# A dense half-group between the two directions' scores of an RWKV-7 scan, and four shared PSUM banks for its small products

## The chip, the cores and the metric

The kernel runs on one core of a Trainium2 chip. Its time is the device time of one execution in microseconds (us), and it was run three times. TensorE is called PE below, VectorE DVE, ScalarE ACT, GpSimd POOL, and SP is the engine that issues most DMAs.

## The reference

One layer of a bidirectional hybrid encoder, 1024 tokens of 1024 channels, float32: half a SwiGLU feed-forward, a mixer, half a second SwiGLU, and a last norm. The mixer projects its input once and feeds two branches, a gated long convolution (Hyena) and an RWKV-7 scan in two directions. Cut to the part that matters here:

```
h = _rmsnorm(x, mix_norm)
u_hy, u_rw, g_hy, g_rw = jnp.split(h @ w_in, split_at, axis=-1)
y_hy = _hyena_branch(u_hy, ...)          # ends in z @ hy_out
y_rw = _rwkv7_branch(u_rw, ...)          # ends in y @ rw_out
merged = jax.nn.sigmoid(g_hy) * y_hy + jax.nn.sigmoid(g_rw) * y_rw
x = x + merged @ w_out

def _rwkv7_step(S, inp):                 # 8 heads of 64, two directions, 1024 steps
    r, w, k, v, kk, a = inp
    sa = jnp.einsum('dbhij,dbhj->dbhi', S, -kk)
    S = S * w[..., None, :] + sa[..., None] * (kk * a)[..., None, :] + v[..., None] * k[..., None, :]
    y = jnp.einsum('dbhij,dbhj->dbhi', S, r)
```

After the scan, the two directions' outputs are added, normed for each head, given a bonus term and multiplied by a gate g.

## The kernel before, in words

The scan is computed in 8 blocks of 128 tokens (`NB`), each two chunks of 64, both directions `d` at once, as products of small matrices. `Rwkv.run` (line 1103) is a Python generator: each `yield` is a place where the caller may put other work of PE. For one block its stretches are, in this order:

- `transposes` of `BT` and the products `pv` for both directions (lines 1141 to 1145), then `ws` with the loads of the next block's `prep`, then `us`, `r` and `ms`;
- `scores` of the next block (line 923): for each direction two pairs of banks, each filled by products of `BK` and `T3` and read by DVE, which multiplies them by a mask into `rw_SC` (line 939); then `eliminate`, some forty short instructions of DVE that invert the triangular parts and end in the transposes of lines 980 and 982, the last writing `rw_xt`;
- `scan`, two chunks with the running state `rw_s`;
- `invert`, in four stretches: three products of `merge` need what ACT or DVE made of the product before (`rw_xt`, `rw_z`, `rw_lt`), and beside them stand the transposes to `rw_AV` and, in the third and fourth, the products of `rates` (tiles `rw_sg` and `rw_tha`) for the block after the next.

All these small products write one-bank tiles of one PSUM pool, `psA` (line 827), taken in turn from 3 buffers: a product that comes to a buffer waits until ACT or DVE has read the tile that was there. PSUM has 8 banks of 2 KB for each partition; the scan's pools hold 5 of them.

PE's other work is long dense matmuls, 128x512. Matmuls of the scan, the gates and Hyena's projection are kept in program order (`InOrder`, line 48), so where the generators yield sets PE's order; the other engines' order is made by a scheduler. Two callers fill the yields:

- `mixer_gates` (line 1362): 32 groups of 24 matmuls into `pw` (pool `mhp`, 3 banks), which yields in the middle and at the end of each, so 64 half-groups of 12; line 1644 takes one step of the scan after each. They last through the scan's preparation, blocks 0 to 4, and the first block's wait for `eliminate`.
- then, for blocks 5, 6 and 7, the loop at line 1655, which after each step of the scan may take a step of `RwkvPost.unit` (norm, bonus and gate of what the scan has finished; four steps a unit; its PSUM tiles come from 2 banks of a pool of their own, `rpp`) and a group of 12 matmuls of `hyena_out` into `pz` (1 bank). The residues of `i` modulo 10 say at which of a block's ten steps each of them stands.

The weights of the dense groups come by DMA into `w_st`, are rounded by ACT into `w_hi` (line 33), and DVE makes the rest, `w_lo` (line 37). ACT reads a finished gate group with a tanh into `mh_o`.

Of the kernel before, what the change touches and what calls it, by code (L numbers as in the profile page):

```python
# [17 lines left out]
PSUM = bass.MemoryType.PSUM  # L18
# [791 lines left out]
class Rwkv:  # L810
# [6 lines left out]
    def __init__(self, tc, ctx, I, dr, ident):  # L817
        self.tc, self.nc, self.I, self.dr, self.ident = tc, tc.nc, I, dr, ident
        self.te = InOrder(tc)
        nc = self.nc  # L820
        pool = lambda name, bufs, **k: ctx.enter_context(tc.tile_pool(name=name, bufs=bufs, **k))
        one = self.one = pool("rw1", 1)
        self.ld = pool("rwl", 2)
        self.el = pool("rwe", 2)
        self.mid = pool("rwm", 2)
        self.tp = pool("rwt", 1)
        self.psa = pool("rwpa", 3, space=PSUM)
        self.pss = pool("rwps", 1, space=PSUM)
        self.psy = pool("rwpy", 1, space=PSUM)

        def const(name, src, *shape):
            t = one.tile([P, *shape], F32, name=name)
            nc.sync.dma_start(t, src)
            return t

        self.w2 = const("rw_w2", I["rw_w2"].rearrange("d r c -> (d r) c"), 512)
        self.a2 = const("rw_a2", I["rw_a2"].rearrange("d r c -> (d r) c"), 512)
        self.start = const("rw_start", I["c_start"], 512)
        self.mask = const("rw_mask", I["c_mask"], 2 * CH)
        self.half = const("rw_half", I["c_half"], 2)  # L840
        self.eye = const("rw_eye", I["c_eye"], 16, 16)
        v = self.vec = one.tile([P, 4, 6], F32, name="rw_vec")
        for j, ap in enumerate((I["rw_w0"][0], I["rw_w0"][1], I["rw_a0"][0], I["rw_a0"][1], I["rw_k_a"])):
            nc.sync.dma_start(v[:, :, j], ap.rearrange("(t p) -> p t", p=P))
        nc.vector.tensor_scalar(v[:, :, 0:5], v[:, :, 0:5], 0.5, None, ALU.mult)
        nc.vector.tensor_scalar(v[:, :, 5], v[:, :, 4], -1.0, 1.0, ALU.mult, ALU.add)
        self.id2 = one.tile([P, CH], F32, name="rw_id2")
        for e in range(2):
            nc.vector.tensor_copy(self.id2[64 * e : 64 * e + 64], ident[64 * e : 64 * e + 64, 64 * e : 64 * e + 64])
        self.PP = [one.tile([P, 8, CH + 1], F32, name=f"rw_pp{d}") for d in range(2)]  # L850
        for t in self.PP:
            nc.vector.memset(t[:, :, 0:1], 1.0)
        self.TT = one.tile([P, 16, CH], F32, name="rw_tt")
        nc.gpsimd.memset(self.TT, 0.0)
        self.Z1 = one.tile([P, 16, 32], F32, name="rw_z1")
        nc.vector.memset(self.Z1, 0.0)
        self.quads = [(e, hb, 64 * e + 32 * hb) for e in range(2) for hb in range(2)]
        self.S = self.mid.tile([P, 8, 64], F32, name="rw_s")
        nc.vector.memset(self.S, 0.0)
# [63 lines left out]
    def scores(self, b):  # L923

        nc = self.nc
        fe = [slice(0, 64), slice(64, 128)]
        m = self.mask.unsqueeze(1).to_broadcast([P, 4, 2 * CH])
        for d in range(2):
# [3 lines left out]
            for h in range(2):  # L932
# [4 lines left out]
                                       T3[fe[e], 4 * h + i, e :: 2 - e], start=True, stop=True)  # L937
                for e in range(2):
                    nc.vector.tensor_tensor(SC[e][:, ts(h, 4)], ps[e], m, ALU.mult)

    def transposes(self, b, d, n):

# [160 lines left out]
    def run(self):  # L1103
# [23 lines left out]
        c = new(0)  # L1127
# [3 lines left out]
            self.prep(c, d)  # L1131
        for _ in range(5):
            yield
        self.scores(c)
        self.eliminate(c)
        for _ in range(5):
            yield
        x = yield from invert(c, 1)
        for s in range(NB):
# [15 lines left out]
            ms()  # L1155
            yield
            if x is not None:
                self.scores(x)
                self.eliminate(x)
                yield  # L1160
            yield from self.scan(c)
            if x is not None:
                c, x = x, (yield from invert(x, s + 2))
# [198 lines left out]
def mixer_gates(tc, I, wp, hA, hctx, hB, dr):  # L1362


    nc, te = tc.nc, InOrder(tc)
    with ExitStack() as ctx:
        pool = lambda name, bufs, **k: ctx.enter_context(tc.tile_pool(name=name, bufs=bufs, side="right", **k))
        ev = pool("mhe", 2)
        pw = ctx.enter_context(tc.tile_pool(name="mhp", bufs=3, space=PSUM))
        for t in range(2):  # L1370
            if t:
                for k in range(KD):
# [207 lines left out]
def hybrid_layer_kernel(ctx: ExitStack, tc: tile.TileContext, I: dict, out: bass.AP):  # L1580
# [58 lines left out]
    early = ExitStack()  # L1639
    right = lambda name, bufs: early.enter_context(tc.tile_pool(name=name, bufs=bufs, side="right"))  # L1640
    with ExitStack() as c2:
        rw = Rwkv(tc, c2, I, dr, ident).run()
        for _ in mixer_gates(tc, I, wp, h0, hctx, hB, dr):
            next(rw)
        with ExitStack() as c3:
            zp, z2, one, work = [right(n, b) for n, b in (("zz1", 1), ("zz2", 1), ("rp1", 1), ("rp2", 1))]
            pz, pq = [c3.enter_context(tc.tile_pool(name=n, bufs=b, space=PSUM)) for n, b in (("zzp", 1), ("rpp", 2))]
            hy = hyena_out(tc, I, wp, zp, z2, pz, dr)
            post = RwkvPost(nc, InOrder(tc), I, dr, ident, one, work, pq)


            todo = [(3, 0), (3, 1), (2, 0), (2, 1), (1, 0), (1, 1)]
            unit = post.unit(3, 0, post.load(3, (0, 2))(0))
            at = 0
            for i, _ in enumerate(rw):
                last = i >= 20
                if last or i % 10 not in (3, 4):
                    next(unit)
                    at += 1
                    if at % 4 == 0:  # L1660
                        b, u = todo[at // 4]
                        unit = post.unit(b, u, post.load(b, (u, 2))(u))
                if i % 10 in ((0, 1, 2, 3) if last else (0, 2, 3, 4, 6, 8)):
                    next(hy)
            for _ in hy:
                pass
# [69 lines left out]
```

## Time and profile before

| what | us |
|---|---|
| median of 3 runs | 2926.61 |
| lowest, highest | 2918.56, 2928.55 |
| the profiled execution's own time | 2928.85 |
| its span, first to last instruction | 2927.1 |
| PE busy | 2726.0 |
| stretch of the scan (from 1365 to 1990 us of the span) | 625 |

The profile is of one execution. Times in its rows are us from the start of the span. In a timeline row the columns are the start, the duration from the first to the last of the merged instructions, the engine, the line (a helper's: L55 is every matmul kept in order, L58 every transpose), the operation, out<-in by tile names (buffer numbers left out, so that `rw_t` can be `rw_t3` or `rw_t`), the shapes, the count, and in brackets how long the engine was idle before it and whom it waited for. A float32 product of the program shows as two in the trace. The granted clock of PE has two levels, 1.0 (2.4 GHz) and 0.5 (1.2 GHz); a stretch shows the mean.

### The profile page before, as it was taken

Reading aid. Unit: us, or ns where it says so; the run is one execution under the profiler, and the core shown is the slowest. Engines: PE = TensorE matmul, PEld = TensorE weight load, DVE = VectorE, ACT = ScalarE, POOL = GpSimd, SP = SyncE. Lnnn points to the kernel's source line nnn. Section 1 sums busy time; section 2 is a strip of 40 time slices with the busy share of each in tenths; the row PEclk is TensorE's granted clock in tenths of the full one; section 3 lists DMA queues with packets and bytes.
Section 4 is the critical chain, followed back from the end, with each engine's and each line's share of the span. In section 5 each row is a group of like instructions: output and inputs, shape, how many; then the busy total and the mean of one; then the engine's idle time right before and its main releaser. Section 6 shows DMA issues by size and latency. Waiting matters only on the chain. (4 is left out here: it accounts for less than half of the span.)

```text
span 2927.1 us, 46056 instructions
## 1 busy us (share of the span) xinstructions
PE 2726.0 (93%) x19440; PEld 2201.1 (75%) x19440; DVE 1235.5 (42%) x2141; ACT 907.8 (31%) x1517; POOL 549.9 (19%) x351
## 2 busy tenths in 40 slices
PE   7999999999688899897899998898999999999998
PEld 6888888888566677775777777675778888888886
DVE  4111010110557769898565556756560111111014
ACT  4111111111445443334444444532332111111112
POOL 2323233232413210000000000000023232323322
PEclk9999999999899999999999998989999999999999
DMA  4111111111442345644435334546731111111102
GB/s 122 51 44 55 40 57 44 40 57 39 142 100 69 105 160 153 174 138 140 125 111 159 101 101 136 155 148 217 207 94 46 55 50 42 53 44 52 47 29 90
DMA packets 408990, 277.49 MB, mean 95 GB/s; under 512 B 51107, under 2 KB 369135, under 8 KB 408144
## 3 DMA queue, kind: packets, MB, share of 16 engines
q1 hardware_dynamic: 408784, 274.55, 31.5%
q8 instruction: 153, 2.51, 0.4%
q14 instruction: 53, 0.43, 0.1%
HBM read 203.58 MB, written 70.91 MB: 94 GB/s over the span
## 5 line engine op out<-in xcount | busy, mean ns | idle before, releaser
L43 PE MATMUL pgu<-hThi,w_hi 128*128 128x512 f32 x1408 | 554.1, 394 | 0.8 <-issue 0.8
L45 PE MATMUL pgu<-hThi,w_lo 128*128 128x512 f32 x1408 | 551.8, 392 | 0.0
L44 PE MATMUL pgu<-hTlo,w_hi 128*128 128x512 f32 x1408 | 547.6, 389 | 0.5 <-DVE hTlo L37 0.3
L210 DVE TENSOR_TENSOR silu<-silu,pgu 128x512 f32<-128x512 f32 x88 | 60.5, 688 | 892.2 <-PE pgu L45 882.7
L33 ACT CAST w_hi<-w_st 128x1024 fp32r<-128x1024 f32 (+1 forms) x180 | 175.2, 974 | 524.6 <-PE pgu L44 320.4
L37 POOL TENSOR_TENSOR w_lo<-w_st,w_hi 128x1024 fp32r<-128x1024 f32 x100 | 240.6, 2406 | 418.5 <-ACT w_hi L33 412.7
L45 PEld LDWEIGHTS pgu<-hThi,w_lo 128*128 128x128 f32 x1408 | 264.4, 188 | 60.6
L44 PEld LDWEIGHTS pgu<-hTlo,w_hi 128*128 128x128 f32 x1408 | 264.5, 188 | 59.6 <-DVE hTlo L37 0.7
L43 PEld LDWEIGHTS pgu<-hThi,w_hi 128*128 128x128 f32 x1408 | 264.6, 188 | 55.0 <-issue 1.2
L43 PE MATMUL pdn<-g_hi,wd_hi 128*128 128x512 f32 x704 | 275.0, 391 | 5.0 <-DVE xT L227 4.5
L45 PE MATMUL pdn<-g_hi,wd_lo 128*128 128x512 f32 x704 | 274.9, 390 | 1.5 <-POOL wd_lo L37 1.5
L44 PE MATMUL pdn<-g_lo,wd_hi 128*128 128x512 f32 x704 | 274.4, 390 | 2.0 <-POOL g_lo L37 2.0
L227 DVE SCALAR_TENSOR_TENSOR xT<-pdn,xT 128x512 f32<-128x512 f32 x192 | 132.4, 690 | 315.4 <-PE pdn L45 315.4
L43 PE MATMUL pw<-hThi,w_hi 128*128 128x512 f32 (+1 forms) x448 | 184.5, 412 | 18.4 <-DVE nm_h L123 10.0
L37 POOL TENSOR_TENSOR wd_lo<-wdst,wd_hi 128x512 fp32r<-128x512 f32 (+1 forms) x112 | 133.3, 1191 | 333.2 <-ACT wd_hi L33 333.2
L45 PE MATMUL pw<-hThi,w_lo 128*128 128x512 f32 (+1 forms) x448 | 184.1, 412 | 12.1 <-DVE w_lo L1226 12.1
L37 POOL TENSOR_TENSOR g_lo<-silu,g_hi 128x512 fp32r<-128x512 f32 x88 | 113.9, 1294 | 397.1 <-ACT g_hi L33 397.1
L44 PE MATMUL pw<-hTlo,w_hi 128*128 128x512 f32 (+1 forms) x448 | 182.5, 407 | 0.0
L33 ACT CAST wd_hi<-wdst 128x512 fp32r<-128x512 f32 (+1 forms) x112 | 64.4, 576 | 379.8 <-PE pdn L44 369.9
L37 POOL TENSOR_TENSOR hTlo<-nm_h,hThi 128x512 fp32r<-128x512 f32 x16 | 23.1, 1445 | 830.2 <-ACT hThi L33 830.2
L43 PEld LDWEIGHTS pdn<-g_hi,wd_hi 128*128 128x128 f32 x704 | 132.2, 188 | 33.7 <-ACT wd_hi L33 4.5
L44 PEld LDWEIGHTS pdn<-g_lo,wd_hi 128*128 128x128 f32 x704 | 132.1, 188 | 30.8 <-POOL g_lo L37 2.9
(312 smaller groups left out, 4253.2 us busy)
## 6 DMA issues: line engine op xcount, KB each, us to landing
w_st<-in_ffn_w_gu SPq DMA_DIRECT2D x88, 512.0 KB
w_st<-in_w_in SPq DMA_DIRECT2D x59, 512.0 KB
wdst<-in_ffn_w_down SPq DMA_DIRECT2D x64, 256.0 KB
wdst<-in_ffn_w_down SPq DMA_DIRECT2D x48, 192.0 KB
d_kf<-kout SPq DMA_DIRECT2D x32, 256.0 KB
hy_k<-d_kf SPq DMA_DIRECT2D x32, 256.0 KB
w_st<-in_w_out SPq DMA_DIRECT2D x16, 512.0 KB
d_X<-sh_x SPq DMA_DIRECT2D x12, 512.0 KB
```

Source lines behind the costliest of these rows:

```text
L33: nc.scalar.copy(hi, src)
L37: eng.tensor_tensor(lo, src, hi.bitcast(F32), ALU.subtract)
L43: te.matmul(out, lhs[0], rhs[0], start=first, stop=False)
L44: te.matmul(out, lhs[0], rhs[1], start=False, stop=False)
L45: te.matmul(out, lhs[1], rhs[0], start=False, stop=last)
L210: nc.vector.tensor_tensor(sl, sl, pu, ALU.mult)
L227: nc.vector.scalar_tensor_tensor(xa, ps, 0.5, xa, ALU.mult, ALU.add)
```

## The change

`scores` becomes a generator that yields after the first direction, so its caller puts a dense half-group between the directions. The gate groups are still 64, and so that their count comes out, the loop around `mixer_gates` takes two steps of the scan at once in five places: at every one the third and fourth stretch of `invert`, which then follow each other. In blocks 5 and 6 the loop's residues go from modulo 10 to 11: Hyena's group that stood after `pv` now stands between the directions; the steps of the norm's units stay at the same stretches of a block. The wait for the first block's `eliminate` has four yields behind it in place of five.

The pool `psA` gets 4 banks, and the norm's units take their tiles from it too, in one turn with the scan's; the gates' pool goes from 3 banks to 2, Hyena's from 1 to 2.

```diff
-        self.psa = pool("rwpa", 3, space=PSUM)
+        self.psa = pool("rwpa", 4, space=PSUM)
...
                 for e in range(2):
                     nc.vector.tensor_tensor(SC[e][:, ts(h, 4)], ps[e], m, ALU.mult)
+            if d == 0:
+                yield
...
-        self.scores(c)
+        yield from self.scores(c)
         self.eliminate(c)
-        for _ in range(5):
+        for _ in range(4):
             yield
...
-                self.scores(x)
+                yield from self.scores(x)
                 self.eliminate(x)
                 yield
...
-        pw = ctx.enter_context(tc.tile_pool(name="mhp", bufs=3, space=PSUM))
+        pw = ctx.enter_context(tc.tile_pool(name="mhp", bufs=2, space=PSUM))
...
+        n = 0
         for _ in mixer_gates(tc, I, wp, h0, hctx, hB, dr):
             next(rw)
+            n += 1
+            if n % 11 == 2 and 2 < n < 68:
+                next(rw)
+                n += 1
...
-            pz, pq = [c3.enter_context(tc.tile_pool(name=n, bufs=b, space=PSUM)) for n, b in (("zzp", 1), ("rpp", 2))]
+            pz = c3.enter_context(tc.tile_pool(name="zzp", bufs=2, space=PSUM))
...
-            post = RwkvPost(nc, InOrder(tc), I, dr, ident, one, work, pq)
+            post = RwkvPost(nc, InOrder(tc), I, dr, ident, one, work, rwkv.psa)
...
-                if last or i % 10 not in (3, 4):
+                if last or i % 11 not in (3, 4, 5):
                     next(unit)
...
-                if i % 10 in ((0, 1, 2, 3) if last else (0, 2, 3, 4, 6, 8)):
+                if i % 11 in ((0, 1, 2, 3) if last else (2, 3, 4, 5, 7, 9)):
                     next(hy)
```

How PE's instructions stand around the scores of an inner block, of before; `rw_bk` marks the scores, one row of 16 for each direction:

```order
L55 MATMUL pw<-hTlo_102,w_hi 128x512
L55 MATMUL pw<-hThi_101,w_lo 128x512
L55 MATMUL psA<-rw_t_9930,rw_bk 128x128 x16
L55 MATMUL psA<-rw_t_10036,rw_bk 128x128 x16
L55 MATMUL pw<-hThi_101,w_hi 128x512
```

And of the changed kernel, at the same place:

```order
L55 MATMUL pw<-hThi_101,w_lo 128x512
L55 MATMUL psA<-rw_t_9915,rw_bk 128x128 x16
L55 MATMUL pw<-hThi_101,w_hi 128x512
L55 MATMUL pw<-hTlo_102,w_hi 128x512
L55 MATMUL pw<-hThi_101,w_lo 128x512
...
L55 MATMUL pw<-hThi_101,w_lo 128x512
L55 MATMUL psA<-rw_t_10017,rw_bk 128x128 x16
L55 MATMUL pw<-hThi_101,w_hi 128x512
```

Twelve dense matmuls stand between the directions now. On PE at the end of `invert`, where `rw_xt,rw_SC` is the third product of `merge` and `rw_t,rw_lt` the fourth, the changed kernel has:

```order
L55 MATMUL psA<-rw_xt,rw_SC_10163 32x32
L55 MATMUL psA<-rl_x,rw_w_8985 128x128 x8
L55 MATMUL psA<-rw_t,rw_lt 32x32 x32
L55 MATMUL psA<-rl_x,rw_a_8987 128x128 x8
L55 MATMUL pw<-hThi_101,w_hi 128x512
```

The twelve dense matmuls that stood before the row of `rw_t,rw_lt` are gone from there. On ACT from the copy of the third product (`rw_lt`) to the copies of the transposed `rw_BT` of an inner block, of before:

```order
L1014 COPY rw_lt<-psA 32x512 x2
L879 ACTIVATE rw_sg<-psA,rw_vec 128x128 x8
L903 ACTIVATE rw_pp_9008<-rw_inc 128x8x64
L904 ACTIVATE rw_inc<-rw_inc 128x512
L1383 ACTIVATE mh_o<-pw 128x512
L903 ACTIVATE rw_pp_9009<-rw_inc 128x8x64
L33 CAST w_hi<-w_st 128x1024
L1023 COPY rw_tt<-psA 32x16x32 x2
L879 ACTIVATE rw_tha<-psA,rw_vec 128x128 x8
L915 ACTIVATE rw_tha<-rw_tha,rw_vec 128x128 x4
L904 ACTIVATE rw_inc<-rw_inc 128x512
L953 COPY rw_BT_11847<-psA 128x512
```

And of the changed kernel (its lines from 941 on are two higher):

```order
L1016 COPY rw_lt<-psA 32x512 x2
L879 ACTIVATE rw_sg<-psA,rw_vec 128x128 x8
L1025 COPY rw_tt<-psA 32x16x32 x2
L903 ACTIVATE rw_pp_9008<-rw_inc 128x8x64
L879 ACTIVATE rw_tha<-psA,rw_vec 128x128 x8
L904 ACTIVATE rw_inc<-rw_inc 128x512
L903 ACTIVATE rw_pp_9009<-rw_inc 128x8x64
L1385 ACTIVATE mh_o<-pw 128x512
L915 ACTIVATE rw_tha<-rw_tha,rw_vec 128x128
L955 COPY rw_BT_10796<-psA 128x512
```

The cast of `w_hi` has left this stretch. On DVE, around the masks of the scores, of the changed kernel (before, the `w_lo` stands ahead of all eight masks):

```order
L1067 TENSOR_TENSOR rw_t_10017<-psA,rw_id_9005 128x8x64
L939 TENSOR_TENSOR rw_SC_11137<-psA,rw_mask 128x512
L939 TENSOR_TENSOR rw_SC_11138<-psA,rw_mask 128x512
L939 TENSOR_TENSOR rw_SC_11137<-psA,rw_mask 128x512
L939 TENSOR_TENSOR rw_SC_11138<-psA,rw_mask 128x512
L37 TENSOR_TENSOR w_lo<-w_st,w_hi 128x1024
L939 TENSOR_TENSOR rw_SC_11178<-psA,rw_mask 128x512
L939 TENSOR_TENSOR rw_SC_11179<-psA,rw_mask 128x512
L939 TENSOR_TENSOR rw_SC_11178<-psA,rw_mask 128x512
L939 TENSOR_TENSOR rw_SC_11179<-psA,rw_mask 128x512
L966 STREAM_TRANSPOSE rw_lt<-rw_a 128x512
```

The `w_lo` now stands between the two directions' masks.

## Rows read from the trace of the kernel before

**Rows 1.** The page, busy us of each engine (share of the span) and instructions.

```profile
PE 2726.0 (93%) x19440; PEld 2201.1 (75%) x19440; DVE 1235.5 (42%) x2141; ACT 907.8 (31%) x1517; POOL 549.9 (19%) x351
```

**Rows 2.** Waits of PE, 1365 to 1990: total us, times, longest.

```profile
PE psA L55 <- DVE rw_SC L939: 24.0, 24, 3.4
PE psA L58 <- ACT rw_BT L953: 5.8, 9, 1.0
```

**Rows 3.** Waits of PE, the first scores alone (1386 to 1400).

```profile
PE psA L55 <- DVE rw_SC L939: 5.2, 3, 3.4
```

**Rows 4.** Waits of PE, five inner blocks (1438 to 1760).

```profile
PE psA L55 <- DVE rw_SC L939: 12.4, 15, 1.5
```

**Rows 5.** Timeline of PE, scores of one inner block.

```profile
1531.50 1.38 PE L55 MATMUL psA<-rw_t,rw_bk 64*128 64x128 f32 x18
1534.34 1.16 PE L55 MATMUL psA<-rw_t,rw_bk 64*128 64x128 f32 x16 [1.45 <-DVE rw_SC L939]
```

**Rows 6.** Timeline of DVE, the same place.

```profile
1532.45 1.23 DVE L37 TENSOR_TENSOR w_lo<-w_st,w_hi 128x1024 fp32r<-128x1024 f32 x1 [3.11 <-ACT w_hi L33]
1533.60 1.28 DVE L939 TENSOR_TENSOR rw_SC<-psA,rw_mask 128x512 f32<-128x512 f32 x2
```

**Rows 7.** Windows of 14 us at scores: busy us, granted clock, DMA share, GB/s.

```profile
1461.00:1475.00 14.00, 11.61 (x100) 9.35 (x101) 8.67 (x13) 4.76 (x10) 0.00 (x0) 0.76 0.21 57
...
1675.00:1689.00 14.00, 11.62 (x134) 9.60 (x133) 8.40 (x13) 4.77 (x10) 0.00 (x0) 0.88 0.21 57
```

**Rows 8.** Timeline of PE, the inner block's `merge`, `rates`, transposes of `BT`, `pv`.

```profile
1488.31 0.76 PE L55 MATMUL psA<-rw_xt,rw_a 32*32 32x16 f32 x68
...
1498.29 1.20 PE L55 MATMUL psA<-rw_xt,rw_SC 32*32 32x32 f32 x64
...
1504.82 1.16 PE L55 MATMUL psA<-rl_x,rw_a 64*128 64x128 f32 x16
...
1508.88 1.05 PE L58 MATMUL psA<-ident,rw_bk 64*128 64x64 f32 x16
...
1512.39 0.27 PE L58 MATMUL psA<-ident,rw_bk 64*128 64x64 f32 x1 [0.99 <-ACT rw_BT L953]
...
1513.75 1.15 PE L55 MATMUL psA<-rw_AV,rw_SC 64*64 64x64 f32 x32 [0.16 <-ACT rw_t L1046]
```

**Rows 9.** Timeline of ACT, the same stretch.

```profile
1499.63 1.17 ACT L1014 COPY rw_lt<-psA 32x512 f32<-32x512 f32 x2
1500.82 2.18 ACT L879 ACTIVATE rw_sg<-psA,rw_vec 128x128 f32<-128x128 f32 x8
...
1505.19 0.59 ACT L1383 ACTIVATE mh_o<-pw 128x512 f32<-128x512 f32 x1
...
1506.20 1.15 ACT L1023 COPY rw_tt<-psA 32x512 f32<-32x512 f32 x2
...
1510.60 1.26 ACT L915 ACTIVATE rw_tha<-rw_tha,rw_vec 128x128 f32<-128x128 f32 x3
1511.77 1.06 ACT L953 COPY rw_BT<-psA 128x512 f32<-128x512 f32 x2
```

**Rows 10.** Window of 14 us at `BT` and `pv`, fifth inner block.

```profile
1721.00:1735.00 14.00, 12.31 (x172) 9.89 (x172) 11.10 (x18) 10.65 (x26) 0.00 (x0) 0.76 0.67 191
```

**Rows 11.** Timeline of DVE, last masks and last instruction of an `eliminate`.

```profile
1470.09 1.29 DVE L939 TENSOR_TENSOR rw_SC<-psA,rw_mask 128x512 f32<-128x512 f32 x2 [1.16 <-PE psA L55]
...
1484.53 0.71 DVE L982 STREAM_TRANSPOSE rw_xt<-rw_t 128x512 f32<-128x512 f32 x1
```

**Rows 12.** Timeline of PE, the first `merge`.

```profile
1415.00 1.17 PE L55 MATMUL psA<-rw_xt,rw_a 32*32 32x16 f32 x120 [1.28 <-DVE rw_xt L982]
```

**Rows 13.** Windows of 16 us at the scores in blocks 5 and 6.

```profile
1816.00:1832.00 16.00, 13.10 (x89) 10.38 (x89) 9.40 (x20) 4.79 (x11) 0.00 (x0) 0.68 0.33 107
1895.00:1911.00 16.00, 12.46 (x109) 9.91 (x110) 11.87 (x22) 7.59 (x14) 0.00 (x0) 0.79 0.36 109
```

**Rows 14.** Timeline of PE, a norm unit's first products in block 6.

```profile
1883.63 1.12 PE L55 MATMUL psA<-rp_y,rp_ones 128*128 128x512 f32 x2 [1.44 <-DVE rp_y L1479]
```

More of the change, by code (lines that the diff above doesn't have):

```diff
@@ L1641, in hybrid_layer_kernel @@
     with ExitStack() as c2:
-        rw = Rwkv(tc, c2, I, dr, ident).run()
+        rwkv = Rwkv(tc, c2, I, dr, ident)
+        rw = rwkv.run()
+        n = 0
         for _ in mixer_gates(tc, I, wp, h0, hctx, hB, dr):
             next(rw)
+            n += 1
+            if n % 11 == 2 and 2 < n < 68:
+                next(rw)
+                n += 1
         with ExitStack() as c3:
             zp, z2, one, work = [right(n, b) for n, b in (("zz1", 1), ("zz2", 1), ("rp1", 1), ("rp2", 1))]
-            pz, pq = [c3.enter_context(tc.tile_pool(name=n, bufs=b, space=PSUM)) for n, b in (("zzp", 1), ("rpp", 2))]
+            pz = c3.enter_context(tc.tile_pool(name="zzp", bufs=2, space=PSUM))
             hy = hyena_out(tc, I, wp, zp, z2, pz, dr)
-            post = RwkvPost(nc, InOrder(tc), I, dr, ident, one, work, pq)
+            post = RwkvPost(nc, InOrder(tc), I, dr, ident, one, work, rwkv.psa)
             todo = [(3, 0), (3, 1), (2, 0), (2, 1), (1, 0), (1, 1)]
@@ L1654, in hybrid_layer_kernel @@
             at = 0
-            for i, _ in enumerate(rw):
-                last = i >= 20
-                if last or i % 10 not in (3, 4):
+            for i, _ in enumerate(rw, n - 69):
+                last = i >= 22
+                if last or i % 11 not in (3, 4, 5):
                     next(unit)
```

## The prediction

> **What bounds the kernel now.** The page comes first: PE is busy for 2726.0 of 2927.1 us and no other engine for half of that [rows 1], so time is won only where PE waits or where its clock is low. The order of instructions changes nowhere before the scan; the page and the timeline then say where in the scan to look, and the waits of PE over its 625 us say for what [rows 2]. First stands the mask of the scores, 24.0 us in 24 waits: 5.2 in the first scores [rows 3], 12.4 in the five inner blocks [rows 4], so 6.4 in the two blocks beside the norm's units. Then come the copies of `rw_BT`, 5.8 us in 9 waits.
>
> The timeline of one inner block shows how the first arises. Scores are 32 products, 64 in the trace, four banks' worth for two directions of two pairs. After 18 the three banks are full, and PE stands for 1.45 us [rows 5]: DVE, itself waiting 3.11 us for `w_hi`, is at a `w_lo` and begins the first mask at 1533.60; two masks take 1.28 [rows 6]. A pair of products takes 1.16, so the masks are the slower of the two and PE waits twice more. Nothing else of PE stands in that stretch, which is why the wait is in full on the path.
>
> The windows show a second cost. In the 14 us from the scores' start the granted clock is 0.76 in two inner blocks, 0.88 in one [rows 7], and 1.00 in the other two: a fall to 1.2 GHz after the second wait. At 0.76, 14 us lose 3.4; at 0.88, 1.7. The five make 8.4 us.
>
> **The change part by part.** No instruction is added or removed on PE; 12 dense matmuls a block move, and buffers change.
>
> *Scores, five inner blocks.* The first direction's four tiles find four banks, and while the half-group (about 2.9 us, from the end of the row at 1504.82 to 1508.88 [rows 8]) runs, DVE masks them: first mask 1.2 after the start, four masks 2.6, so done at 3.8, when the second direction starts at 2.3 + 2.9 = 5.2. No product waits for a bank. The 12.4 go, and with them what made the clock fall, 8.4: -20.8. Lower bound of the gain: the idle alone, -12.4.
>
> *What stood between the third and fourth product of `merge`.* The half-group hid the copy of the third product. Count from the third product's end (1498.29 + 1.20 = 1499.49). The copies end at +1.3 [rows 9]; the products of `rates`, 1.16 long [rows 8], hide nearly all of that: 0.1 a block. But ACT now gets to the transposes' copies in less time. From the copies to `rw_tt` at 1506.20 to the end of the first copy of `rw_BT`, half of the 1.06 from 1511.77, it took 6.1 us [rows 9]. That stretch now starts at +3.5 (when the first eight tanh end), has an exponential (I take 0.6) and `mh_o` (0.59) more and two `rw_tha` steps (0.4 each) less: the first copy of `rw_BT` ends at about +10. PE comes there sooner: +1.3, the fourth product 1.2, `rates` 1.2, the half-group 3.0, the transposes 0.7 (an estimate: the 15 of them that follow each other in a row of 1.05 with a wait in it) and `pv` 1.15 make 8.5. With four banks the first pair of transposes and `pv` find room; the second pair's second bank is the first one's, so one wait of 1.5 remains, where there were 0.99, 0.16 and smaller ones, and the end of `pv` is at +11.9. Before it was 1513.75 + 1.15 = +15.4, with one half-group more; without it 12.4. So -0.5 a block, less 0.1: -2.0 for five. Bounds: ACT a us earlier, -7; two us later, +8.
>
> The Trainium skill says in "TensorE: Matmul & The Clock Gate" (HAM oscillation — how this bites in real kernels) that once a kernel's matmuls followed each other without long waits, double-buffering PSUM gave no further gain. By that the fourth bank alone would be worth nothing here, and the sum would be 2.5 us smaller; the row of 5.8 us speaks for some worth, as those waits are for a bank.
>
> *The clock there.* At `BT` and `pv` it fell in two of the five inner blocks, 3.4 us in the last [rows 10] and 1.7 in the one before, 5.0 together. One wait of 1.5 is as long as the wait at 1534.34 [rows 5], which with its followers brought falls in three blocks of five. I count three, of 3.4 each: +5.2 against now. Bounds: none, -5.0; all five, +12.
>
> *`eliminate`.* It hangs on the second direction's masks, and these now stand behind a `w_lo`, whose `w_hi` waits until the half-group between the directions has freed a buffer: a cast over the same columns (about 1.1, an estimate from the `w_lo` of 1.23) and the `w_lo`, so masks from 2.3 to 4.9 after the second direction's start, 2.6 after its end. Now they end at 1471.38, some 0.9 after the products [rows 11]. `rw_xt` thus comes 1.7 later; it ended at 1485.24 and PE wanted it at 1488.31 [rows 8], 3.1 of slack, of which some 1.0 came of a half-group at the low clock (this is the block of the window of 0.76). What is left is 0.4: no wait by the rows, for which I put +1 in all. Upper bound: in the slower rival.
>
> *The first scores.* PE already waits 1.28 for `rw_xt` behind them [rows 12]. The first mask stays late, as DVE is still at `prep`; the masks end about 3.3 earlier, so does `eliminate`, and the first `merge` starts 3.3 earlier. PE then waits some 5 us there in one piece, for which I count a fall of the clock of 3.4: 0. Bounds -8 (5.2 of waits and the clock's part) and +4.
>
> *Blocks 5 and 6.* The scores lose 6.4 of waits and, by the windows, 16 x 0.32 + 16 x 0.21 = 8.5 of clock [rows 13]. Against this, the group after `pv` has moved, and PE comes 3.0 earlier to the norm unit's first products, which DVE does not have ready: in block 6 PE already waits 1.44 there [rows 14]. I count all of it as wait, 6.0 for both, one fall of the clock, 3.4, and 1.0 for `eliminate`, which has more `w_lo` and `z_sg` in it: -14.9 + 10.4 = -4.5. Sharing the four banks in turn with the units can hold a product until DVE reads a unit's tile, and can spare one that waited for a third bank; I take nothing for it. Bounds -12 and +5.
>
> *Smaller pools for the gates.* With two banks, a group begins after the tanh of the group before last, 0.59 long and due a whole group earlier: nothing.
>
> The sum is -20.8 - 2.0 + 5.2 + 1.0 + 0 - 4.5 = -21.1. It stands against the profiled execution's 2928.85 (span 2927.1 and 1.75 around it), so 2907.7; that execution lies 2.24 over the median of the three, so the forecast is 2905.5, own range 2899 to 2912.
>
> **The rivals.**
>
> *The low clock stays with the small products.* The waits go from the scores to `BT` in every block and to the norm units in two, and each brings a fall: two more of 3.4 in the inner blocks, one more in the tail, +10.2, thus 2915.7. For it: falls at `BT` in two blocks already. Against: three inner blocks with the same waits have none. The Trainium skill describes this under "A second HAM failure mode: psum-queue depth-cycling" of "TensorE: Matmul & The Clock Gate": short idle spells between groups that cycle through PSUM banks make the clock swing. That the fourth bank and the moved group shorten these spells at the scores, but leave one at `BT`, is as the rows say.
>
> *All falls but today's at `BT` go.* Then 5.2, and the 3.4 of the tail and of the first scores, are not lost: -12.0, thus 2893.5. For it: the inner blocks without falls; against: the new waits are in one piece.
>
> *The wait only moves.* If ACT is 2 us later at `rw_BT` than I have it, PE waits 3.5 there, +10 in five blocks, and the falls come in all: about +8 more. 2923.5, within the noise. For it: ACT is busy for 11 of 14 us there. Against: the cast of `w_hi`, 1.0 us, has left the stretch.
>
> *Slower: `eliminate` is late.* If the `w_lo` between the masks waits as it did at 1532.45, 3.11 us, on top of what I have, `rw_xt` is 2.7 late in seven blocks, with a fall each: 7 x (2.7 + 3.4) = 43 against the -21, thus about 2927, no gain; at 4.0 late it is 7 x 7.4 = 52, and 2936. The lateness decides from the slack of 0.4 on, and the kernel is slower from 2.7. Against: that wait ended with a group of PE, which I have already counted.
>
> **How the numbers follow.** Forecast 0.44, low clock stays 0.19, more gain 0.19, wait only moves 0.12, slower 0.06. About 0.3%, 8.8 us, can be told from no change. Faster by that (under 2917.8) are the forecast, the larger gain, three quarters of the low-clock case and a little of the next: 0.79. Slower 0.06, the rest 0.15. The range leaves out the ends of the first and the last two cases: 2886 to 2921.
>
> **What would show it.** The row of waits for `rw_SC` falls from 24.0 to under 4. PE shows a wait of about 1.5 for `rw_BT` in each inner block, and about 0.1 before the fourth product of `merge`. The first `merge` starts near 1412 after a wait of 4 to 6. Waits for `rp_y` in blocks 5 and 6 grow by about 3 each. The five windows at the scores have a clock of 1.00. The forecast is wrong if waits for `rw_xt` appear in the inner blocks, or if the clock over the scan stays as low as now.

## The result and the profile after

The changed kernel takes 2897.47 us (median of 4 runs, 2895.29 to 2905.31) against 2926.49 before (4 runs, 2918.56 to 2928.55): a ratio of 0.9916, 95% interval 0.9894 to 0.9939. In a later set of runs it took 2897.31 against 2926.72, ratio 0.9910 (0.9891 to 0.9929). The forecast was 2905.5: the direction is right and the gain is 29 us where 21 were forecast. That is 1.5 under the forecast's own range of 2899 to 2912, and inside the wide one of 2886 to 2921.

The profile of after is of the slowest of its four runs, 2905.31. Its lines from 941 on stand two lower than before's, so that line 982 is now 984. The stretch of the scan, from the first gate product to the scan's last product, is 595.9 us where it was 624.1: 28.2 less. The rest of the span is 4.6 longer (2903.5 - 595.9 against 2927.1 - 624.1); in the second profile of the same kernel it is 2303.1, as before, so these 4.6 are spread and not the change.

The waits of PE over the scan, which answer to [rows 2] (total us, times, longest):

```profile
PE psA L55 <- DVE rp_y L1481: 7.8, 3, 4.1
PE psA L55 <- DVE rw_xt L984: 7.3, 2, 6.4
PE psA L55 <- issue: 6.4, 7, 2.3
PE psA L58 <- issue: 6.3, 2, 4.3
PE pz L55 <- ACT w_hi L33: 4.9, 1, 4.9
PE psA L58 <- ACT rw_BT L955: 4.9, 4, 1.2
PE pw L55 <- ACT mh_o L1385: 2.1, 1, 2.1
```

The row for `rw_SC` is gone, all 24.0 us of it. In its place three waits have come or grown that the reader should note: one of 6.4 for `rw_xt`, which the prediction had at 4 to 6, and one of 4.9 for `w_hi` and one of 2.1 for `mh_o`, which it did not have. Of the 7.8 for `rp_y`, 4.1 lie behind the scan's last product. The waits that the trace puts down to nothing ("issue") have grown as well, at `psA` from 6.0 to 12.7; the last experiment comes back to the larger part of them.

The timelines of PE and of DVE at the scores of an inner block, as [rows 5, 6] (the dense matmuls between the rows are left out):

```profile
1524.06 2.06 PE L55 MATMUL psA<-rw_t,rw_bk 64*128 64x128 f32 x32
...
1529.01 2.06 PE L55 MATMUL psA<-rw_t,rw_bk 64*128 64x128 f32 x32
```

```profile
1525.25 2.48 DVE L939 TENSOR_TENSOR rw_SC<-psA,rw_mask 128x512 f32<-128x512 f32 x4 [3.36 <-PE psA L55]
1529.96 1.23 DVE L37 TENSOR_TENSOR w_lo<-w_st,w_hi 128x1024 fp32r<-128x1024 f32 x1 [2.23 <-ACT w_hi L33]
1531.11 2.48 DVE L939 TENSOR_TENSOR rw_SC<-psA,rw_mask 128x512 f32<-128x512 f32 x4
```

Both directions run through; the first mask starts 1.2 after the first product, and the second direction's masks begin 2.1 after its start behind a `w_lo`, as forecast. The windows at the five inner scores, which answer to [rows 7] (us, PE busy, granted clock, DMA share, GB/s), show no fall; the first and the last of five equal rows:

```profile
1460.00:1474.00 14.00, 14.00 (x218) 1.00 0.21 59
...
1727.00:1741.00 14.00, 14.00 (x217) 1.00 0.19 59
```

At `BT` and `pv`, as [rows 8], one wait stands, here and in three more of the five blocks (1.21 to 1.24; the fifth ran at the low clock just before and shows none). The clock behind it stays at 1.00:

```profile
1503.64 0.27 PE L58 MATMUL psA<-ident,rw_bk 64*128 64x64 f32 x1
1505.15 0.71 PE L58 MATMUL psA<-ident,rw_bk 64*128 64x64 f32 x15 [1.24 <-ACT rw_BT L955]
1505.79 1.15 PE L55 MATMUL psA<-rw_AV,rw_SC 64*64 64x64 f32 x32
```

```profile
1505.10:1510.10 5.00, 4.95 (x67) 1.00 0.71 229
```

The two ends look worse than forecast. Ahead of the first scores PE waits for a bank of the gates' pool, behind them for `rw_xt`, and in block 6 for `w_hi`:

```profile
1386.55 0.50 PE L55 MATMUL pw<-hThi,w_hi 128*128 128x512 f32 x1 [2.11 <-ACT mh_o L1385]
...
1418.42 0.78 PE L55 MATMUL psA<-rw_xt,rw_a 32*32 32x16 f32 x44 [6.39 <-DVE rw_xt L984]
...
1886.56 0.80 PE L55 MATMUL pz<-s_hi,w_hi 128*128 128x512 f32 x1 [4.91 <-ACT w_hi L33]
```

### The profile page after: what moved, and what is told of

It reads as the page before. It is cut to its first block, busy times and chain, and to the rows that moved or that the text cites. A ratio compares the mean times of both kernels' runs of the same rounds, so it can differ in the third digit from the quotient of the medians.

```text
span 2903.5 us, 46061 instructions
## 1 busy us (share of the span) xinstructions
PE 2718.3 (94%) x19440; PEld 2198.2 (76%) x19440; DVE 1232.0 (42%) x2141; ACT 905.1 (31%) x1517; POOL 555.4 (19%) x351
## 5 line engine op out<-in xcount | busy, mean ns | idle before, releaser
L45 PE MATMUL pw<-hThi,w_lo 128*128 128x512 f32 (+1 forms) x448 | 186.8, 418 | 12.1 <-DVE w_lo L1228 12.1
```

Of the source, the lines that this page charges most:

```text
L45: te.matmul(out, lhs[1], rhs[0], start=False, stop=last)
```

## The experiments

My theory was the prediction's: the half-group between the directions removes the wait for the masks, and the fourth bank is worth some 2.5 us. The rival: the bank removes it, and the half-group is worth little. The next table is worked out from the timelines of all kernels below. Its stretches run from the first gate product of the scan to the first `merge` (the first row of `rw_xt,rw_a`), from there to the sixth `merge`, which are the five inner blocks, and from there to the scan's last product (us). Cut there, a stretch holds the same number of gate half-groups in every kernel (11, 50 and 3), and in the second one PE has the same instructions in the same order in all kernels with the half-group between the directions, and in all without it. In brackets stands what the clock cost: half of the time that the stretch ran at 1.2 GHz. That is an upper bound, since PE stands idle in some of it.

| kernel | time, median | to the first `merge` | five inner blocks | from there to the end |
|---|---|---|---|---|
| before | 2926.5 | 49.4 (5.1) | 356.2 (15.4) | 218.5 (22.2) |
| order alone | 2924.63 | 48.8 (2.0) | 349.8 (8.3) | 218.6 (15.4) |
| banks alone | 2899.74 | 47.5 (3.4) | 336.0 (6.8) | 208.5 (13.7) |
| banks, first scores early | 2899.81 | 47.6 (5.1) | 333.1 (1.7) | 211.4 (20.5) |
| changed | 2897.47 | 49.0 (5.4) | 332.2 (11.6) | 214.6 (20.5) |
| changed, again | 2897.31 | 48.5 (5.1) | 327.1 (6.9) | 215.6 (17.1) |
| changed, tail as before | 2892.65 | 48.4 (5.1) | 329.8 (10.3) | 212.3 (22.2) |
| changed, first scores early | 2893.33 | 45.3 (3.4) | 328.3 (5.1) | 215.2 (17.1) |
| changed, early, tail as before | 2886.35 | 44.9 (3.4) | 323.9 (1.7) | 215.2 (23.9) |
| the same, the units' own bank | 2896.79 | 45.3 (3.4) | 331.4 (10.2) | 217.8 (20.5) |

One profile of each kernel goes into this, and the same instructions take unequal times: in the inner blocks the two profiles of the changed kernel differ by 5.1, and the six rows from "changed" on lie between 323.9 and 332.2. Most of that is the clock. Without the brackets the six lie between 319.6 and 323.2, the banks without the half-group at 329.2 and 331.4, before at 340.9, the order alone at 341.6. The largest single piece is a fall of 10.2 us in block 2 behind waits for DMAs, which three of the six profiles have and three have not:

```profile
1560.94 0.65 PE L55 MATMUL pw<-hThi,w_hi 128*128 128x512 f32 x1 [1.33 <-DMA hThi<-d_hB_hi]
```

So a difference of a few us in a whole stretch says little of an edit, unless the clock's part is taken off.

**The order alone.**

```diff
-        self.psa = pool("rwpa", 4, space=PSUM)
+        self.psa = pool("rwpa", 3, space=PSUM)
-        pw = ctx.enter_context(tc.tile_pool(name="mhp", bufs=2, space=PSUM))
+        pw = ctx.enter_context(tc.tile_pool(name="mhp", bufs=3, space=PSUM))
...     # Hyena 1 bank, the norm's units 2 of their own
```

> The changed order with the pools of before (psA 3 banks, gates 3, Hyena 1, the norm's units 2 of their own). Theory A (the order needs the fourth bank): with m3|m4 together, both rates products want two of three banks, so the second waits for eight tanh of the first (about 1.3 a block), the transposes to BT and pv then wait for the second's tanh (3 to 4 a block more than in the changed kernel), and the first direction's fourth tile still waits for a mask (about 1 a block). That is 5 to 6 us in each of five blocks: 2918 to 2930, no gain over before. Waits for rw_sg and rw_tha appear in the inner blocks, waits for rw_SC fall to 4 to 8. Rival B (the half-group between the directions is what pays, the bank little): 2905 or less, waits for rw_sg and rw_tha under 5 us in all.

2924.63, ratio 0.9995 (0.9980 to 1.0010): no gain. Theory A's result, but not all by its mechanism. Waits of PE over the five inner blocks, in this kernel:

```profile
PE psA L55 <- DVE rw_SC L939: 10.1, 10, 1.5
PE psA L58 <- ACT rw_BT L955: 5.6, 10, 1.1
PE psA L55 <- ACT rw_sg L879: 2.7, 5, 0.5
PE psA L55 <- ACT rw_tha L879: 1.3, 4, 0.3
```

I had put the waits for `rw_SC` at 4 to 8 over the whole scan and those at `BT` 15 to 20 higher in the inner blocks; they are 19.8 over the scan (10.1 here) and 5.6. With three banks each direction still stops, half-group or not:

```profile
1526.58 1.38 PE L55 MATMUL psA<-rw_t,rw_bk 64*128 64x128 f32 x18
1528.52 1.16 PE L55 MATMUL psA<-rw_t,rw_bk 64*128 64x128 f32 x14 [0.56 <-DVE rw_SC L939]
...
1532.56 1.38 PE L55 MATMUL psA<-rw_t,rw_bk 64*128 64x128 f32 x18
1535.40 1.16 PE L55 MATMUL psA<-rw_t,rw_bk 64*128 64x128 f32 x14 [1.46 <-DVE rw_SC L939]
```

The same 18 products as in [rows 5], then a stop. One thing the half-group does do on its own: the windows at the scores of this kernel all have a clock of 1.00, though the wait of 1.46 is as long as the one of before.

```profile
1526.00:1540.00 14.00, 11.98 (x109) 1.00 0.22 58
```

**The banks alone**: the kernel before with the pools of the change and nothing moved.

```diff
-        self.psa = pool("rwpa", 3, space=PSUM)
+        self.psa = pool("rwpa", 4, space=PSUM)
...     # mhp 2, zzp 2, the norm's units from psa
```

> The order of before with the pools of the change. Theory A: the fourth bank alone lets the first direction pass and leaves a wait of 1.3 to 1.5 in the second (masks are 0.64 each and start late), so waits for rw_SC go from 24 to 9 to 14; waits for rw_BT go from 5.8 to under 2, since the half-group between the third and fourth product of merge still stands; less 4 us at the first gate groups from their two banks. Time 2908 to 2916, so some half of the gain. Rival B (the bank is worth nothing without the moved group): 2920 to 2927, waits for rw_SC over 18.

2899.74, ratio 0.9909 (0.9888 to 0.9931): better than theory A's 2908 to 2916, and as fast as the changed kernel within the intervals. The theory of the prediction falls here: 27 us come without moving anything. The four pools changed in one edit, though. In the inner blocks (356.2 to 336.0) only the scan's and the gates' pool bear on it; behind them (218.5 to 208.5) Hyena's second bank and the shared turn do too, and which of these brings how much of that was not tried by itself. Its scores, and DVE and the clock at them:

```profile
1530.07 2.06 PE L55 MATMUL psA<-rw_t,rw_bk 64*128 64x128 f32 x32
1532.91 2.95 PE L55 MATMUL psA<-rw_t,rw_bk 64*128 64x128 f32 x32 [0.78 <-DVE rw_SC L939]
```

```profile
1531.03 1.23 DVE L37 TENSOR_TENSOR w_lo<-w_st,w_hi 128x1024 fp32r<-128x1024 f32 x1 [3.10 <-ACT w_hi L33]
1532.17 4.87 DVE L939 TENSOR_TENSOR rw_SC<-psA,rw_mask 128x512 f32<-128x512 f32 x8
```

```profile
1530.00:1544.00 14.00, 13.07 (x210) 1.00 0.22 58
```

The first direction has its four banks; after that PE follows DVE, mask by mask. There is one visible wait of 0.78 in each block (5.6 for `rw_SC` over the whole scan, where I had expected 9 to 14), and the second direction takes 2.95 instead of 2.06, so the masks cost 1.7 a block (0.78 + 0.89) where they cost 2.4 to 2.6. What it saves besides is the clock: no fall at the scores of the five inner blocks, where three had one. At `BT`, where I expected the waits gone, they are longer: 7.7 in five blocks, up to 1.7.

**The half-group again, on four banks.** Two pairs tell its price apart from the tail's. First the changed kernel with the tail in the order of before:

```diff
-                yield from self.scores(x)
+                for _ in self.scores(x):
+                    if s < 5:
+                        yield
...     # the residues of the tail modulo 10, as before
```

> The changed kernel, but blocks 5, 6 and 7 in the order of before (no yield between the directions for the last two scores, the residues modulo 10), with the shared four banks. The trace of the changed kernel shows the tail, from the scores of block 6 on, 4.4 shorter than before. Theory A (the moved group gives that): 2900 to 2904, with waits of 1 to 1.5 for rw_SC in two blocks and the rp_y waits back at about 1.4. Rival B (what the scores gain is given back at w_hi, 4.9 us, and at rp_y; the 4.4 came from the banks): the same time as the changed kernel or less, 2891 to 2898.

2892.65, ratio 0.9887 (0.9863 to 0.9910): rival B. The tail's gain comes of the banks: it is there in the order of before too (218.5 to 208.5 with the banks alone). Its new order saves nothing: from the sixth `merge` on PE stands idle for 16 to 20 us in the four profiles with shared banks and the order of before, for 25 to 29 in the three with the new order. That the new order costs time is not shown, since the stretch itself takes 208.5 to 215.2 and 214.6 to 215.6, and the clock's part varies by more. PE's waits in this kernel's tail have 4.3 for `rp_y` where the changed kernel has 7.8, none of 4.9 for `w_hi`, 3.8 for `w_lo` where that has 2.2, and only 1.1 for `rw_SC`. The `w_hi` at 1886.56 is late in the changed kernel because Hyena's group between the directions brings the next `s_hi` and `s_lo` into ACT and DVE at the time of the masks: ACT's cast waits for the DMA of `w_st`, and that is issued at 1882.97, when DVE has ended the first `s_lo`. Against the banks alone this kernel has the half-group in blocks 0 to 4 only: 7.1 us less, though the two intervals overlap.

Then the first scores, earlier:

```diff
-        for d in range(2):
-            self.prep(c, d)
-        for _ in range(5):
+        self.prep(c, 0)
+        yield
+        self.prep(c, 1)
+        for _ in range(2):
             yield
         yield from self.scores(c)
         self.eliminate(c)
-        for _ in range(4):
+        for _ in range(6):
```

> The changed kernel with prep of the second direction issued one half-group later and three half-groups fewer ahead of the first scores in all (two of them now behind eliminate; the count of yields is the same). Theory A (the 6.4 us for rw_xt and the 2.1 us for mh_o, each with its fall of the clock, are idle time that better placed dense groups fill): rw_xt under 1.5, mh_o gone, 8 us of waits and 5 to 7 of clock less, some 2 for a wait ahead of the second direction: 2885 to 2890. Rival B (DVE's prep sets when the scores can start, so the wait only moves ahead of the scores): 2894 to 2899, with a wait of 4 or more for rw_bk.

2893.33, ratio 0.9890 (0.9869 to 0.9911): 4 us, between the theories. Both waits have shrunk, to 0.31 and 1.21, and a new one of 1.83 for `prep` stands ahead of the scores:

```profile
1384.88 0.46 PE L55 MATMUL psA<-rw_t,rw_bk 64*128 64x128 f32 x2 [1.83 <-ACT rw_inc L904]
1385.64 3.64 PE L55 MATMUL psA<-rw_t,rw_bk 64*128 64x128 f32 x30 [0.31 <-ACT mh_o L1386]
1392.47 2.95 PE L55 MATMUL psA<-rw_t,rw_bk 64*128 64x128 f32 x32 [0.22 <-DVE rw_SC L939]
...
1413.32 0.85 PE L55 MATMUL psA<-rw_xt,rw_a 32*32 32x16 f32 x82 [1.21 <-DVE rw_xt L984]
```

The first products now run at the low clock (3.64 for 30 of them, where 32 take 2.06), behind that wait.

Both edits together, the banks with the earlier scores but no half-group anywhere, and the changed kernel once more beside them:

> The changed kernel itself, on the same chip as the next two, to compare with them. Both theories: 2894 to 2900.

> The earlier first scores and the tail in the order of before together, with the four shared banks and the half-group between the directions in blocks 0 to 4. The two alone gave 4.1 and 4.8 less than the changed kernel in their medians. Theory A (they are in different stretches, so they add): 2886 to 2891. Rival B (they were the spread of the clock's falls and not the order): 2893 to 2898.

> The banks of the change in the order of before, no half-group between the directions anywhere, with the earlier first scores. Theory A (the banks carry the gain, the moved half-group 3 to 4 us in the five inner blocks): 2890 to 2896, 3 to 5 behind the kernel with the half-group. Rival B (the half-group is worth nothing once the banks are there): the same as that kernel within 2.

2897.31 (0.9910, 0.9891 to 0.9929), 2886.35 (0.9865, 0.9845 to 0.9885) and 2899.81 (0.9913, 0.9895 to 0.9931). The two edits add in the medians, theory A, and this is the fastest version found: 11 us under the changed kernel, 40 under before, 0.9865 of it. In its one profile the tail's part does not show: 215.2, as with the earlier scores alone. The last two kernels differ only in where the half-groups stand: between the directions, in blocks 0 to 4 and at the first scores, or where they stood before. Their intervals do not touch: 13.5 us. The table shows 8.1 of it in the scan: 9.2 in the inner blocks, with the same cost of the clock (1.7), and 2.7 ahead of them, but 3.8 lost behind them, of which 3.4 are the clock's. I had expected 3 to 5. Without a half-group between them the early first scores gain nothing, since the masks are late there and the second direction waits 2.71 for them:

```profile
1390.12 4.23 PE L55 MATMUL psA<-rw_t,rw_bk 64*128 64x128 f32 x32 [2.71 <-DVE rw_SC L939]
```

**The clock behind the wait for `BT`.** The prediction counted three falls there; the profile after has none. So ACT repeats a copy ahead of the one that PE waits for:

```diff
+        if n == "BT" and d == 0 and b["s"] < 5:
+            for _ in range(b["s"]):
+                nc.scalar.copy(dst[0], ps[0])
         for e in range(2):
             nc.scalar.copy(dst[e], ps[e])
```

> The changed kernel, but ACT repeats the first copy of rw_BT of the first direction s times in block s (0 to 4), about 0.53 each, so that PE's wait there grows from 1.2 by half a us a block to some 3.4. Theory A (how long the engine idles decides whether the clock falls; 1.2 is on the safe side, and the before kernel's falls came of two or three waits in a row): no fall in blocks 0 and 1, falls of 3.4 or more right behind the wait in blocks 2, 3 and 4. Rival B (the length of a single wait up to 3.4 does not decide): no falls in any block behind that wait, or falls in blocks 0 and 1 as often as in 3 and 4. Time some 5 us of waits and 2 to 6 of clock over the changed kernel.

The wait did not grow block by block: only one repeat came ahead of the copy of the second bank, and that bank was the one handed on, since the first stayed busy. But it grew once, from 1.21 to 1.70 or 1.72, in three blocks (block 2 ran at the low clock just before, for another reason, and shows no wait). In the rows below the first is of block 0, the others of blocks 1, 3 and 4; under them are the windows from these rows on.

```profile
1438.65 0.71 PE L58 MATMUL psA<-ident,rw_bk 64*128 64x64 f32 x15 [1.21 <-ACT rw_BT L958]
...
1502.48 0.71 PE L58 MATMUL psA<-ident,rw_bk 64*128 64x64 f32 x15 [1.72 <-ACT rw_BT L958]
...
1643.41 0.83 PE L58 MATMUL psA<-ident,rw_bk 64*128 64x64 f32 x15 [1.72 <-ACT rw_BT L958]
...
1708.44 0.95 PE L58 MATMUL psA<-ident,rw_bk 64*128 64x64 f32 x15 [1.70 <-ACT rw_BT L958]
```

```profile
1438.60:1443.60 5.00, 4.95 (x67) 1.00 0.67 220
1502.40:1507.40 5.00, 4.92 (x54) 0.66 0.61 194
1643.40:1648.40 5.00, 4.84 (x54) 0.66 0.51 182
1708.40:1713.40 5.00, 4.93 (x55) 0.66 0.61 208
```

Half a us more, and the clock fell to 1.2 GHz in three of three, for 3.4 us each (2902.81, a single run). In the changed order and its variants 23 waits of 1.20 to 1.24 in six profiles (this block 0 among them) brought none. That is theory A, though the falls came with waits of 1.7 already, where I had expected them from 2.2 on. It holds for this order only: in the two kernels in the order of before with four banks, eight waits of 1.67 to 1.75 brought one fall. There a half-group stands between the third and the fourth product of `merge`, so that what PE did before the wait is not the same. Whether that is the reason was not tried.

**Three tries beyond.** All start from the fastest version.

```diff
+            if n == "BT" and d == 0 and e == 0:
+                nc.vector.tensor_copy(dst[e], ps[e])
...     # the other copies by ACT, as they were
```

> The best kernel so far (earlier first scores, tail in the order of before: 2886.4), but DVE and not ACT makes the first of the two copies of rw_BT of the first direction. Theory A (PE's 1.2 us there is ACT being late, with tanh, exponentials and a mh_o ahead of the copy; DVE is free earlier): waits for rw_BT fall from 6.1 to under 2, nothing takes their place: 2880 to 2883. Rival B (the wait moves on to the copies of pv, or DVE's prep is late for it at the next scores): 2885 to 2889.

2894.58 (2886.90 to 2896.91), ratio 0.9880 (0.9846 to 0.9915): no gain over the 0.9865 (0.9845 to 0.9885) of the version that it starts from, and by the intervals no loss that can be told. PE's wait is 1.22 as before, for the copy that ACT kept, and DVE comes to its own only at 1432.59, behind `prep`:

```profile
1432.74 0.71 PE L58 MATMUL psA<-ident,rw_bk 64*128 64x64 f32 x15 [1.22 <-ACT rw_BT L958]
```

```profile
1431.99 0.68 DVE L909 SCALAR_TENSOR_TENSOR rw_t<-rl_kh,rw_pp 64x512 f32<-64x512 f32 x1
1432.59 0.68 DVE L956 COPY rw_BT<-psA 128x512 f32<-128x512 f32 x1
```

```diff
+            next(hy)
             for i, _ in enumerate(rw):
...
-                if i % 10 in ((0, 1, 2, 3) if last else (0, 2, 3, 4, 6, 8)):
+                if i != 2 and i % 10 in ((0, 1, 2, 3) if last else (0, 2, 3, 4, 6, 8)):
```

> The same kernel as a base, but Hyena's first group stands ahead of block 5's transposes to rw_BT, where the gate groups have run out and PE waits 1.7 for rw_tt and 1.5 for rw_tha, and the group ahead of that block's scores, which waits 2.4 for its w_lo, is left out there (the count of groups is the same). Theory A (a dense group in the wrong place leaves one wait uncovered and makes another): 5.6 of waits and 3 to 5 of clock less: 2877 to 2883. Rival B (the first group needs z split into s_hi and s_lo, 4 us of ACT and 5 of DVE, so PE waits there for it instead): 2885 to 2890, with a wait of 3 or more for s_lo.

2891.17 (2885.59 to 2894.39), ratio 0.9870 (0.9830 to 0.9910): no gain either, rival B's result. The waits of 1.7, 1.5 and 2.4 became one of 7.08 for `w_hi`. The split of `z` is not what ends it: ACT has cast the last `s_hi` by 1765.4, and its cast of `w_hi` then waits for the DMA of the weights.

```profile
1769.70 0.80 PE L55 MATMUL pz<-s_hi,w_hi 128*128 128x512 f32 x1 [7.08 <-ACT w_hi L33]
```

```profile
1769.03 0.62 ACT L33 CAST w_hi<-w_st 128x512 fp32r<-128x512 f32 x1 [1.07 <-DMA w_st<-in_hy_out]
```

> The last two edits together. Theory A for both: 2872 to 2879. If only one of them holds, its own time.

2897.25 (2894.44 to 2901.05), ratio 0.9895 (0.9862 to 0.9928): no gain from both together.

Last, the shared turn by itself. The prediction took "nothing" for it, but behind block 5's scan PE stands for 2.2 to 4.3 us in the middle of 16 transposes to `rw_AV`, in every kernel so far whose norm's units take their tiles from `psA`, and the trace names nothing that it waits for there ("issue"). In the kernel before and in the order alone, where the units have their own banks, the stop at that place is 0.8 or none; a second one a block later, of 1.8 to 2.2, is there too.

```diff
-            pz = c3.enter_context(tc.tile_pool(name="zzp", bufs=2, space=PSUM))
+            pz, pq = ...     # one bank each
-            post = RwkvPost(nc, InOrder(tc), I, dr, ident, one, work, rwkv.psa)
+            post = RwkvPost(nc, InOrder(tc), I, dr, ident, one, work, pq)
```

> The fastest version (2886.4) with Hyena's groups on one bank and the norm's units on one bank of their own, so that the scan alone turns over its four. Theory A (sharing in turn costs nothing that can be told, as the prediction took it, while a unit wants two tiles at once and Hyena's next group the bank that DVE still reads): 2888 to 2896, with new waits for rp_y, rp_k or z_sg. Rival B (the scan's products are held up by the units' tiles in the shared turn, among them the 3.2 us in the transposes of rw_AV that the trace puts down to nothing): that stop falls under 1 us, and the time to 2878 to 2884.

2896.79 against 2919.83 of before in the same rounds, ratio 0.9920 (0.9898 to 0.9943), where sharing had 0.9865: slower, and 0.8 over theory A's range. PE's waits in the tail with sharing, and below without:

```profile
PE psA L58 <- issue: 5.0, 2, 3.2
PE psA L55 <- DVE rp_y L1484: 4.5, 2, 4.0
```

```profile
PE psA L55 <- DVE rp_y L1509: 7.5, 5, 2.7
PE psA L55 <- DVE rp_y L1490: 4.6, 5, 1.2
PE psA L55 <- DVE rp_y L1484: 3.0, 1, 3.0
```

The 5.0, both stops, are gone. The larger one, 3.2, goes with the shared turn, as rival B had it, though PE now waits 2.74 for `rp_y` a few us ahead of that place, so that it comes there later; of the smaller one it is not shown, since kernels without sharing have it too. The units' two tiles on one bank wait 12.1 (7.5 + 4.6) for DVE. But little of the 10 us lies where the edit is: from the sixth `merge` on it is 2.6, or 6.0 without the clock's part, and 7.5 lie in the inner blocks, where both programs have the same instructions on every engine and the clock cost 10.2 against 1.7. So sharing costs some waits and in these two profiles saves more, 3 to 6 us; since Hyena's groups went from two banks to one in the same edit, how much of that is sharing's own is not shown.

## Why the prediction was right, and where it was not

*Scores.* The waits went as forecast, 12.4 to nothing, and the clock there is 1.00 in all five windows. But the cause was wrong in the main, and that the sum came out near is luck in part, as both changes were made at once. The step that failed is the one by which DVE masks the four tiles while the half-group runs: it stood as the reason for the 20.8, and the fourth bank was put at 2.5 us. Order alone: nothing that can be told from before. Banks alone: 27 us. The half-group is worth something once the banks are there: 6 to 12 us in the inner blocks without the clock's part, 7 to 14 by the medians of the variants. In the changed kernel itself 2 of it are left against the banks alone: by the table 4 to 9 are won in the inner blocks and 6 to 7 lost behind them, 3 to 7 of these by the clock.

I had read the row of 18 products followed by 1.45 of idle [rows 5] and looked for work to put into the idle time; the row itself says that the third bank was the last, and that the rest of the second pair would run if there were one more.

The Trainium skill, in "TensorE: Matmul & The Clock Gate" (HAM oscillation — how this bites in real kernels), tells of a kernel whose loop was rearranged so that PE stays warm, and to which double-buffering PSUM then gave no further gain. This case's runs differ, 0.9909 for the banks alone, and the measurement decides: PE waited 24.0 us for banks here [rows 2]. Whether PE waited for banks in that other kernel, the Trainium skill does not say.

*The clock at* `BT`. This is the term that was mis-sized: +5.2 from three assumed falls, measured as none, so -5.0 against before. The wait came out at 1.21 to 1.24 and not at 1.5, and waits half a us longer brought falls. The five inner blocks went from 356.2 to 332.2, -24.0, where the terms for them add up to -16.6. This term alone makes 10.2 more; the 2.8 that it gives too much are lost elsewhere, above all to the fall of 10.2 us in block 2, which costs up to 5.1, behind waits for the DMAs of `hThi` and `hTlo` (2.9 in all, 1.9 before). The second profile, without that fall, has 327.1, -29.1.

*Between the third and the fourth product of* `merge`: 0.1 a block forecast, one wait of 0.2 in the whole scan. *`eliminate`*: no wait for `rw_xt` in any inner block, so the slack of 0.4 held.

*The first scores and the smaller pools.* The forecast had the first `merge` 3.3 earlier and 3.4 of clock behind it, 0 in all. From the scan's start to the first `merge` it took 49.4 before and takes 49.0 (48.5 in the second profile), so that most of the 3.3 did not come. The "nothing" for the smaller pools of the gates fails: ACT comes to `mh_o` at 1385.92 after twelve instructions of `prep` and a load of its table, 16.5 after the scan's start. Before it was as late, 16.4, and with three banks no product waited for it; now PE stands for 2.1, and a fall of 3.4 us follows. The wait for `rw_xt` is 6.4 (I had 4 to 6) with a fall of 10.2 us, of which 6.2 lie behind the wait and cost 3.1, near the forecast's 3.4. The earlier scores show that some 4 us lay there.

*Blocks 5 and 6.* From the sixth merge to the end: 218.5 to 214.6, -3.9 (-2.9 in the second profile) for a forecast of -4.5. But this too is a sum of things I had not separated: the order of before with the four banks takes 208.5 to 215.2. The waits for `rp_y`, which I had growing by 3.0 in each of two blocks, grew in block 6 alone, from 1.44 to 2.87, and to 7.57 in the second profile. The wait of 4.9 for `w_hi` was not forecast.

*The rivals.* "All falls but today's at `BT` go" (2893.5) comes near in time, and half of what it says happened; the tail and the first scores kept their falls. "`eliminate` is late" and "the wait only moves" did not happen in the changed kernel. The first of these is added up wrong in the prediction: 43 us set against the gain of 21 make 2948.5 and not 2927, and 52 make 2957.5; its seven falls of 3.4 alone would have used up the gain. "The low clock stays with the small products" is what the longer wait shows could have happened, for half a us.

## What to carry to other kernels

When PE stops after a count of products that just fills a pool, try one more bank there, taken from a pool whose tiles live long, before reordering the program; run the two halves of such a change apart, since together they show only their sum. A bank taken away is paid for where the reader is late, so look at what stands ahead of that reader's instruction at the busiest place of its engine, here ACT at `mh_o`. Treat the slack of a single wait as a cost to be known: here 1.2 us brought no fall of the clock in 23 waits, and half a us more three of three, though one of eight in the other order. Before a stretch of one kernel is compared with that of another, see that both hold the same instructions, and take off what the clock cost in each: here the same instructions took 323.9 to 332.2.

## What was not expected of the hardware

A wait's length does not settle by itself whether the clock falls. At the scores 1.45 followed by 0.57 and 0.37 to 0.57 with no dense matmul between brought a fall in three of five blocks; 0.56 and 1.46 with a half-group between them, 2.0 in all where those make 2.4 to 2.6, in none of five. At `BT` waits of 0.99 with smaller ones beside them brought two of five before, 1.09 with one of 0.2 behind it one of four in the order alone, single ones of 1.2 none of 23.

A wait that the profile puts down to "issue" can be one that comes with a pool: the stop of 3.2 us in the transposes to `rw_AV` was not there when the norm's units had a bank of their own. What the eleventh transpose needed and the ten ahead of it did not, the trace does not show; that stays open.
